# A transformer layer's start on one core: first loads, first modulation and first input stage in an order written by hand, and three router folds spread out

## The chip, the cores and the metric

The kernel runs on one core of one Trainium2 chip. Its engines are TensorE (PE in the rows, with its weight loads as PEld), VectorE (DVE), ScalarE (ACT), GpSimd (POOL) and SyncE (SP), which here only issues loads; 16 DMA engines move the data. The metric is the device time of one execution in microseconds, taken as the median of several runs.

## The reference

One layer works on x, 256 rows by 2048 columns, in float32, with a conditioning vector c of 2048:

```python
mod = silu(c) @ w_ada + b_ada                       # 6 vectors of 2048
shift1, scale1, gate1, shift2, scale2, gate2 = split(mod, 6)
h = layer_norm(x) * (1 + scale1) + shift1
q, k, v, su, sv, ga, gb = split(h @ w_in)           # 1024 columns each, ga and gb 2048
out_a = stick_breaking_attention(q, k, v)           # 8 heads of 128
out_b = gelu(su) * (mask(sgu_w) @ layer_norm(gelu(sv)) + sgu_b)
merged = sigmoid(ga) * (out_a @ w_proj_a) + sigmoid(gb) * (out_b @ w_proj_b)
x = layer_norm(alpha * x + gate1 * (merged @ w_out), ln1)
h = layer_norm(x) * (1 + scale2) + shift2
y = moe(h)    # 32 experts in 4 groups; one group, two of its experts for each row
return layer_norm(alpha * x + gate2 * y, ln2)
```

## The kernel before

All of it is one function, `trunk_kernel`, with helpers inside. Weights come in chunks of 128 x 2048 float32 (1 MB) through the tiles `ring` (four; in the input stages two more, `ringa`), each issued by `chunk` on SP's queue. SP and POOL issue in the order in which the code is written. PE, ACT and DVE get their order from a scheduler, up to the attention heads, where the order is written out too.

A product in float32 is made of three products of reduced parts (`mm3`, lines 203 to 205): `split` casts a chunk on ACT to the high part `wh` (line 194) and subtracts on DVE to the low part `wl` (line 195). `split_out` (lines 199 and 200) does the same with the transposed, modulated x, which becomes `hT`.

**Start.** `turn_x` loads the two halves of x, takes their statistics (line 161), normalizes them (line 182) and transposes them on PE by `pt` (line 187) into `nT`. Shift and scale of the first modulation come from chunks of w_ada in `ada_part`: the shift (`v` = 0) as a chain of multiply-adds into `comp` on DVE (lines 264 and 266), summed over partitions by PE's `pg<-ones` (line 274); the scale (`v` = 1) on PE, `pg<-ring,csg` (line 262), copied by ACT (line 271) and gathered by `pcols<-quart`. Both end with line 276 on DVE, which adds the bias column `bcol`. They are called `sh` and `sc` in the rows. Line 304 applies them to `nT`.

**Input projection.** `in_stage` runs over five groups of the 16 blocks of 128 in the inner dimension: (0, 1), (2, 3), 4 to 7, 8 to 11, 12 to 15. Each stage goes through five targets in turn, `sv` (kept in PSUM), `sut`, `qT`, `kT` and `vt`, with PSUM tiles `a` added to or copied to the target by `park` (lines 294 and 296). Between them it yields, and the caller pulls so many steps of the next stage's shift and scale as the tables PACE0 to PACE3 say:

```python
for kts, ahead, pace in (((0, 1), ada_half(1), PACE0), ((2, 3), ada_stage(1), PACE2), ...):
    for i, _ in enumerate(in_stage(kts)):
        pull(pace[i])
```

**After it** come spatial gating and attention, the two branch projections with their gates, the output projection into `y`, the norm, the routing and the experts, whose weights stream through the same tiles up to the end. In the output projection (16 chunks; group `g` of 4, step `q` of 4) three folds prepare the router's weights `wr`: `fold_shift` (lines 609 to 611: `pr<-sh,wr`, then wr times the scale), `fold_scale` (lines 616 to 618: `pr<-l1c,wr`, then wr times the norm's gain) and `fold_rows` (some transposes).

Of the kernel before, what the change touches and what calls it, by code (L numbers as in the profile page):

```python
# [9 lines left out]
F32R = mybir.dt.float32r  # L10
# [20 lines left out]
ADA3 = (2, 1, 0, 0, 1, 1, 0, 1, 1, 1)  # L31
ADAM = (1, 1, 1, 1, 1, 1, 1, 1, 2, 1, 1, 1, 1, 1, 1, 1)
ADAO = (1, 1, 1, 1)
PACE0 = (2, 2, 0, 0, 0, 0, 0, 0, 0, 0)
PACE1 = (1, 1, 1, 0, 1, 1, 1, 2, 1, 0)
PACE2 = (0, 2, 2, 1, 1, 0, 1, 1, 1, 0)
PACE3 = (1, 1, 2, 0, 2, 0, 1, 1, 1, 0)
# [6 lines left out]
def trunk_kernel(ctx, tc, x, c_t, w_ada1, w_ada2, b_ada, b_adac, w_in, sgu_wt, sgu_b, sgu_ln, w_pr, w_o, w_r, b_r,  # L44
# [9 lines left out]
    def m8(name, dt=F32):  # L54
        return wk.tile([128, D], dt, name=name, tag="m8", bufs=NM8)
# [40 lines left out]
    S.dma_start(cact, c_t)  # L96

    bcol = cp.tile([128, 6 * KT], F32, name="bcol")
    S.dma_start(bcol, b_adac)
    brc = cp.tile([36, 1], F32, name="brc")  # L100
    S.dma_start(brc, b_r)
    lnc = cp.tile([128, 2, G], F32, name="lnc")
    S.dma_start(lnc, sgu_ln)
    wr = cp.tile([128, KT, 36], F32, name="wr")
    S.dma_start(wr, w_r)
    l1c = cp.tile([128, 3, KT], F32, name="l1c")
    S.dma_start(l1c[:, 0:2], ln1_c)
    ones = cp.tile([128, 128], F32, name="ones")
    V.memset(ones, 1.0)
    V.memset(l1c[:, 2:3], 1.0)  # L110
# [40 lines left out]
    V.memset(ecol[0:1, 1:2], 1e6)  # L151
    csg = cp.tile([128, KT], F32, name="csg")
    S.activation(csg, cact, AF.Silu)
    V.tensor_scalar(bcol[:, KT:2 * KT], bcol[:, KT:2 * KT], 1.0, None, op0=ALU.add)
    V.tensor_scalar(bcol[:, 4 * KT:5 * KT], bcol[:, 4 * KT:5 * KT], 1.0, None, op0=ALU.add)


    def stats(parts, name):
# [12 lines left out]

    nT = [m8(f"nT{i}") for i in range(2)]

    def turn_x():
        X = []
        for n in range(NT):
            t = m8(f"x{n}")
            nc.sync.dma_start(t, x[n * 128:(n + 1) * 128])
            X.append(t)
        for n in range(NT):  # L180
            mv = stats(blocks(X[n]), f"x{n}")
            V.tensor_scalar(X[n], X[n], mv[:, 0:1], mv[:, 2:3], op0=ALU.subtract, op1=ALU.mult)
        for kp in range(8):
            pt = pb(f"pt{kp}")
            for k in range(2):
                for n in range(NT):
                    TE.transpose(pt[:, k * 256 + n * 128:k * 256 + (n + 1) * 128],
                                 X[n][:, (2 * kp + k) * 128:(2 * kp + k + 1) * 128], ident)
            S.copy(nT[kp // 4][:, (kp % 4) * 512:(kp % 4 + 1) * 512], pt)


    def split(w):
        wh, wl = w8("wh", F32R), w8("wl", F32R)
        S.copy(wh, w)  # L194
        V.tensor_sub(wl, w, wh)  # L195
        return wh, wl
# [15 lines left out]

    w_at = [0]

    def in_chunk():
        i = w_at[0]
        w_at[0] += 1
        return split(chunk(w_in[i]))

    def row_part(accs, parts, kts, w, c0, first, last):  # L220

# [26 lines left out]

    cols = {n: cp.tile([128, KT], F32, name=n) for n in ("sh1", "sc1", "sh2", "sc2")}

    def ada_part(v, src, k0, wd):

        pg = pb(f"pg{v}")
        comp = k2(f"comp{v}")[:, :wd]
        for i, a in enumerate(src):
            w = chunk(a)
            for k in range(D // wd):
                kt = D // wd * i + k
                col, ws = csg[:, kt:kt + 1], w[:, wd * k:wd * (k + 1)]
                if v == 1:  # L260
                    j = kt % 4
                    TE.matmul(pg[32 * j:32 * j + 32, :wd], col.to_broadcast([128, 32]), ws, start=kt < 4, stop=kt >= 12)
                elif kt == 0:
                    V.tensor_scalar(comp, ws, col, None, op0=ALU.mult)
                else:
                    V.scalar_tensor_tensor(comp, ws, col, comp, op0=ALU.mult, op1=ALU.add)
            if i < len(src) - 1:
                yield
        nb = wd // 128
        if v == 1:  # L270
            S.copy(comp, pg[:, :wd])
            pg = pb("pcols")
        for b in range(nb):
            TE.matmul(pg[:, b:b + 1], comp[:, b * 128:(b + 1) * 128], quart if v == 1 else ones[:, 0:1],
                      start=True, stop=True)
        V.tensor_add(cols["sc1" if v == 1 else "sh1"][:, k0:k0 + nb], pg[:, 0:nb],
                     bcol[:, v * KT + k0:v * KT + k0 + nb])
        yield

    def ada_half(f):  # L280
        for v in range(2):
            yield from ada_part(v, [w_ada1[v, 0, 2 * f + c] for c in range(2)], 2 * f, 256)

    def ada_stage(s):
        for v in range(2):
            yield from ada_part(v, [w_ada1[v, s, c] for c in range(4)], 4 * s, 512)

    vt, sut, qT, kT_ = m8("vt"), m8("sut"), m8("qT"), m8("kT")
    vtv = vt.rearrange("p (n c) -> p n c", n=NT)
    sva = [[pa(f"sv{g}{n}") for n in range(NT)] for g in range(2)]  # L290

# [6 lines left out]
    def in_stage(kts):  # L298

        w = D // len(kts)  # L300
        first, last = kts[0] == 0, kts[-1] == KT - 1
        for kt in kts:
            t = nT[kt // 8][:, (kt % 8) * 256:(kt % 8 + 1) * 256]
            V.tensor_scalar(t, t, cols["sc1"][:, kt:kt + 1], cols["sh1"][:, kt:kt + 1], op0=ALU.mult, op1=ALU.add)
            split_out(hT(hh, kt), hT(hl, kt), t)
        for dst in (None, sut, qT, kT_, vtv):
            for g in range(2):
                c0 = g * 512 % w
                if c0 == 0:
                    parts = in_chunk()  # L310
                if dst is None:
                    row_part(sva[g], parts, kts, w, c0, first, last)
                else:
                    accs = [pb(f"a{g}{n}") for n in range(2)]
                    if dst is vtv:
                        row_part(accs, parts, kts, w, c0, True, True)
                    else:
                        col_part(accs, parts, kts, w, c0)
                    for n in range(2):
                        park(dst[:, n, g * 512:(g + 1) * 512] if dst is vtv else  # L320
                             dst[:, (2 * g + n) * 512:(2 * g + n + 1) * 512], accs[n], first)
                yield
# [4 lines left out]
    def ada_steps():  # L327
        for v in (2, 3, 4, 5):
# [4 lines left out]
            for h in range(2):  # L333
# [19 lines left out]
                else:  # L353
                    for b in range(8):
                        TE.matmul(pg[:, b:b + 1], acc[:, 128 * b:128 * (b + 1)], ones[:, 0:1], start=True, stop=True)
                    V.tensor_add(cols["sh2" if v == 3 else "sc2"][:, 8 * h:8 * h + 8], pg[:, 0:8],
                                 bcol[:, v * KT + 8 * h:v * KT + 8 * h + 8])
                yield

    ada_it = ada_steps()  # L360
# [1 line left out]
    def ada_step(n=1):  # L362
        for _ in range(n):
            next(ada_it, None)

    turn_x()
    for _ in ada_half(0):
        pass

    def grow(extra):  # L370
        nonlocal ring
# [10 lines left out]
    def pull(n):  # L382
        for _ in range(n):
            next(ahead, None)

    more = [m8(f"ringa{i}") for i in range(NMORE)]
    grow(more)
    for kts, ahead, pace in (((0, 1), ada_half(1), PACE0), ((2, 3), ada_stage(1), PACE2),
                             (range(4, 8), ada_stage(2), PACE1), (range(8, 12), ada_stage(3), PACE3)):
        for i, _ in enumerate(in_stage(kts)):  # L390
            pull(pace[i])
    shrink(more)
    sgu = m8("sgu")
    wst = sgu[:, :1024].rearrange("p (g t) -> p g t", g=G)
# [231 lines left out]
    for g in range(4):  # L626
        accs = [pa(f"y{g}{n}") for n in range(NT)]
        for q in range(4):
# [6 lines left out]
                        wh[:, s], wl[:, s], kt == 0, kt == KT - 1)  # L635
            ada_step(ADAO[g])
            if g < 2 and q in (1, 3):
                (fold_shift, fold_scale, fold_rows, int)[2 * g + q // 2]()
        if g < 3:
            for n in range(NT):  # L640
                residual(g, n, accs[n])
# [573 lines left out]
```

## Time and profile before

| | |
|---|---|
| median of 3 runs | 1629.26 us (1628.90 to 1630.96) |
| profiled execution, its own time | 1632.55 us |
| its span | 1630.9 us |
| mean granted TensorE clock | 0.908 of full speed |
| busy: PE, PEld, DVE, ACT, POOL | 1382.5, 862.0, 808.5, 388.9, 56.6 us |
| DMA | 576.15 MB, mean 353 GB/s |

Times in rows count from the span's start. PE's busy time takes in matmuls that overlap, so it says where PE had work, not how fast it was. The shares are means over stages with different limits.

### The profile page before, as it was taken

Reading aid. Unit: us, or ns where it says so; the run is one execution under the profiler, and the core shown is the slowest. Engines: PE = TensorE matmul, PEld = TensorE weight load, DVE = VectorE, ACT = ScalarE, POOL = GpSimd, SP = SyncE. Lnnn points to the kernel's source line nnn. Section 1 sums busy time; section 2 is a strip of 40 time slices with the busy share of each in tenths; the row PEclk is TensorE's granted clock in tenths of the full one; section 3 lists DMA queues with packets and bytes.
Section 4 is the critical chain, followed back from the end, with each engine's and each line's share of the span. In section 5 each row is a group of like instructions: output and inputs, shape, how many; then the busy total and the mean of one; then the engine's idle time right before and its main releaser. Section 6 shows DMA issues by size and latency. Waiting matters only on the chain. (4 is left out here: it accounts for less than half of the span.)

```text
span 1630.9 us, 24878 instructions
## 1 busy us (share of the span) xinstructions
PE 1382.5 (85%) x10266; PEld 862.0 (53%) x10267; DVE 808.5 (50%) x1114; ACT 388.9 (24%) x521; POOL 56.6 (3%) x76
## 2 busy tenths in 40 slices
PE   4999999999999998994898698697697797797663
PEld 3879889898999996773423123133133133232111
DVE  6777879788788776877424113123123122132105
ACT  2522335564333332324201001001001001001002
POOL 0000000002000110000100000000000000000000
PEclk9899999999999998996999699799699799798777
DMA  8968878578989888883899999999999999999992
GB/s 323 356 255 315 335 275 302 178 246 310 347 321 338 318 309 333 309 340 163 342 421 420 422 421 420 422 421 420 421 420 421 421 421 421 421 420 421 421 421 123
DMA packets 80351, 576.15 MB, mean 353 GB/s; under 512 B 9448, under 2 KB 9448, under 8 KB 10600
## 3 DMA queue, kind: packets, MB, share of 16 engines
q1 hardware_dynamic: 78624, 569.41, 87.7%
q10 hardware_dynamic: 1608, 5.10, 0.8%
q8 instruction: 81, 1.33, 0.3%
q14 instruction: 38, 0.31, 0.0%
HBM read 572.38 MB, written 2.10 MB: 352 GB/s over the span
## 5 line engine op out<-in xcount | busy, mean ns | idle before, releaser
L195 DVE TENSOR_TENSOR wl<-ring,wh 128x2048 fp32r<-128x2048 f32 x95 | 217.6, 2292 | 25.8 <-ACT wh L194 25.7
L194 ACT CAST wh<-ring 128x2048 fp32r<-128x2048 f32 x95 | 180.9, 1906 | 148.3 <-DMA ring<-in_w_in 62.3
L937 DVE TENSOR_TENSOR hb<-sg,pgun 128x128 f32<-128x128 f32 x28 | 8.0, 287 | 329.8 <-ACT sg L936 329.8
L994 DVE TENSOR_TENSOR y<-pdn,comp 32x512 f32<-32x512 f32 x112 | 76.9, 687 | 186.7 <-PE pdn L973 185.5
L342 DVE SCALAR_TENSOR_TENSOR acc<-ring,csg,acc 128x1024 f32<-128x1024 f32 x120 | 153.6, 1280 | 6.1 <-DMA ring<-in_w_ada 4.5
L936 ACT ACTIVATE sg<-pgun 128x128 f32<-128x128 f32 x28 | 7.8, 277 | 610.6 <-PE pgun L930 610.6
L203 PE MATMUL a<-hT,wh 128*128 128x256 f32 x384 | 110.8, 289 | 0.0
L204 PE MATMUL a<-hT,wh 128*128 128x256 f32 x384 | 109.2, 285 | 0.0
L205 PE MATMUL a<-hT,wl 128*128 128x256 f32 x384 | 108.4, 286 | 0.0
L930 PE MATMUL pgun<-ringm,misc 128*32 128x256 f32 x1024 | 76.1, 437 | 17.6 <-DMA ringm<-in_w_gu 17.6
L1086 PE MATMUL po<-y,sl 128*128 128x512 f32 x112 | 64.2, 738 | 27.2 <-DVE sl L918 27.2
L930 PE MATMUL pgun<-ringw,misc 128*32 128x256 f32 x960 | 72.5, 441 | 16.8 <-DMA ringw<-in_w_gu 16.8
L930 PE MATMUL pgun<-ring,misc 128*32 128x256 f32 x992 | 69.9, 421 | 13.7 <-DMA ring<-in_w_gu 13.6
L205 PE MATMUL gb<-hT,wl 128*128 128x256 f32 x256 | 73.6, 287 | 7.5 <-DVE wl L195 7.5
L203 PEld LDWEIGHTS a<-hT,wh 128*128 128x128 f32 x384 | 74.5, 194 | 6.3 <-issue 3.6
L205 PEld LDWEIGHTS a<-hT,wl 128*128 128x128 f32 x384 | 73.8, 194 | 1.9 <-DVE sut L296 0.8
L204 PEld LDWEIGHTS a<-hT,wh 128*128 128x128 f32 x384 | 74.6, 194 | 0.4 <-issue 0.2
L205 PE MATMUL ga<-hT,wl 128*128 128x256 f32 x256 | 73.0, 285 | 1.1 <-DVE wl L195 1.1
L203 PE MATMUL ga<-hT,wh 128*128 128x256 f32 x256 | 72.8, 284 | 0.0
L203 PE MATMUL gb<-hT,wh 128*128 128x256 f32 x256 | 72.8, 284 | 0.0
L204 PE MATMUL gb<-hT,wh 128*128 128x256 f32 x256 | 72.4, 283 | 0.0
L204 PE MATMUL ga<-hT,wh 128*128 128x256 f32 x256 | 72.4, 283 | 0.0
(404 smaller groups left out, 2604.0 us busy)
## 6 DMA issues: line engine op xcount, KB each, us to landing
ring<-in_w_ada SPq DMA_DIRECT2D x87, 1024.0 KB, 5.9
ring<-in_w_gu SPq DMA_DIRECT2D x66, 1024.0 KB, 19.8
ringw<-in_w_gu SPq DMA_DIRECT2D x64, 1024.0 KB, 19.8
ringm<-in_w_gu SPq DMA_DIRECT2D x64, 1024.0 KB, 19.8
ring<-in_w_in SPq DMA_DIRECT2D x63, 1024.0 KB, 6.5
ringm<-in_w_down SPq DMA_DIRECT2D x32, 1024.0 KB, 19.9
ringw<-in_w_down SPq DMA_DIRECT2D x32, 1024.0 KB, 19.9
ring<-in_w_down SPq DMA_DIRECT2D x32, 1024.0 KB, 19.8
```

Source lines behind the costliest of these rows:

```text
L194: S.copy(wh, w)
L195: V.tensor_sub(wl, w, wh)
L203: TE.matmul(acc, lh, rh, start=first, stop=False)
L204: TE.matmul(acc, lh, rl, start=False, stop=False)
L205: TE.matmul(acc, ll, rh, start=False, stop=last)
L342: V.scalar_tensor_tensor(acc, ws, c, acc, op0=ALU.mult, op1=ALU.add)
L930: TE.matmul(acc[m * j:m * j + m, :2 * f].rearrange("p (a f) -> p a f", a=2), x[:, 2 * c + k], w[:, :, f * j:f * (j + 1)], start=i + k == 0 ...
L936: S.activation(sg[:, :w], acc[:, :w], AF.Silu)
L937: V.tensor_mul(hb[:, :w], sg[:, :w], acc[:, w:2 * w])
L994: V.tensor_mul(y4[32 * el:32 * el + 32, 512 * n:512 * (n + 1)], pdn[32 * n:32 * n + 32, :], gate2[0][32 * n:32 * n + 32, :])
L1086: TE.matmul(po, sl[:, n * 128:(n + 1) * 128], y4[:, 512 * b:512 * (b + 1)], start=True, stop=True)
```

## The change

The loads of `bcol`, `brc`, `lnc`, `wr` and `l1c` leave ACT's queue for SP's: `bcol` behind the first four chunks of w_ada, the others behind the first two chunks of w_in. These two chunks go to the tiles of `kT` and `vt`, which hold nothing yet (`early`). The 1 that was added to two sixths of `bcol` ahead of all is added at the end of each sum instead. From the work on x to the end of the first input stage, PE, ACT and DVE follow the order of the code (`begin`): chunk one of the shift, both chunks and the end of the scale, chunk two and the end of the shift. `in_stage` casts its first chunk before it modulates x and splits each next chunk one step ahead (`coming`); `ada_half` does the scale before the shift; PACE0 spreads the pulls. The folds move from the steps (g, q) = (0, 1), (0, 3), (1, 1) to (0, 1), (1, 1), (1, 3).

```diff
-PACE0 = (2, 2, 0, 0, 0, 0, 0, 0, 0, 0)
+PACE0 = (0, 1, 0, 1, 1, 1, 0, 0, 0, 0)
...
-    S.dma_start(bcol, b_adac)
-    S.dma_start(brc, b_r)
-    S.dma_start(lnc, sgu_ln)
-    S.dma_start(wr, w_r)
-    S.dma_start(l1c[:, 0:2], ln1_c)
...
-    V.tensor_scalar(bcol[:, KT:2 * KT], bcol[:, KT:2 * KT], 1.0, None, op0=ALU.add)
-    V.tensor_scalar(bcol[:, 4 * KT:5 * KT], bcol[:, 4 * KT:5 * KT], 1.0, None, op0=ALU.add)
...
-        return split(chunk(w_in[i]))
+        return split(early.pop(0) if early else chunk(w_in[i]))
...
-            w = chunk(a)
+            w = a if any(a is t for t in held.values()) else chunk(a)
...
-        V.tensor_add(cols["sc1" if v == 1 else "sh1"][:, k0:k0 + nb], pg[:, 0:nb],
-                     bcol[:, v * KT + k0:v * KT + k0 + nb])
+        V.scalar_tensor_tensor(cols["sc1" if v == 1 else "sh1"][:, k0:k0 + nb], pg[:, 0:nb], float(v == 1),
+                               bcol[:, v * KT + k0:v * KT + k0 + nb], op0=ALU.add, op1=ALU.add)
...
     def ada_half(f):
-        for v in range(2):
+        for v in (1, 0):
...
+        w0 = early.pop(0) if first else chunk(w_in[w_at[0]])
+        w_at[0] += 1
+        wh, wl = w8("wh", F32R), w8("wl", F32R)
+        S.copy(wh, w0)
         for kt in kts:
             t = nT[kt // 8][:, (kt % 8) * 256:(kt % 8 + 1) * 256]
             V.tensor_scalar(t, t, cols["sc1"][:, kt:kt + 1], cols["sh1"][:, kt:kt + 1], op0=ALU.mult, op1=ALU.add)
             split_out(hT(hh, kt), hT(hl, kt), t)
+        V.tensor_sub(wl, w0, wh)
+        coming, left = (wh, wl), 10 * 512 // w
         for dst in (None, sut, qT, kT_, vtv):
             for g in range(2):
                 c0 = g * 512 % w
                 if c0 == 0:
-                    parts = in_chunk()
+                    parts, left = coming, left - 1
+                    coming = in_chunk() if left else None
...
-    turn_x()
-    for _ in ada_half(0):
-        pass
...
+    nc.sync.dma_start(X[0], x[:128])
+    nc.sync.dma_start(X[1], x[128:])
+    held = {(v, c): chunk(w_ada1[v, 0, c]) for v, c in ((0, 0), (1, 0), (0, 1), (1, 1))}
+    nc.sync.dma_start(bcol, b_adac)
+    for t, src in ((kT_, w_in[0]), (vt, w_in[1])):
+        nc.sync.dma_start(t, src)
+        early.append(t)
+    begin = ExitStack()
+    begin.enter_context(tc.manual_schedule(engines={E.PE, E.Activation, E.DVE}))
+    turn_x()
+    shift, scale = [ada_part(v, [held[v, c] for c in range(2)], 0, 256) for v in range(2)]
+    next(shift)
+    next(scale)
+    next(scale)
+    next(shift)
+    nc.sync.dma_start(lnc, sgu_ln)
+    nc.sync.dma_start(wr, w_r)
+    nc.sync.dma_start(l1c[:, 0:2], ln1_c)
+    nc.sync.dma_start(brc, b_r)
     more = [m8(f"ringa{i}") for i in range(NMORE)]
     grow(more)
     for kts, ahead, pace in (((0, 1), ada_half(1), PACE0), ((2, 3), ada_stage(1), PACE2),
                              (range(4, 8), ada_stage(2), PACE1), (range(8, 12), ada_stage(3), PACE3)):
         for i, _ in enumerate(in_stage(kts)):
             pull(pace[i])
+        begin.close()
...
-                (fold_shift, fold_scale, fold_rows, int)[2 * g + q // 2]()
+                (fold_shift, int, fold_scale, fold_rows)[2 * g + q // 2]()
```

The changed kernel's lines are numbered a little lower (276 is 271 there, 262 is 257, 195 is 186). In the orders below a row is a line of the kernel, the operation, its output and inputs, and the output's shape; x8 counts equal rows, and the number behind a name tells one use of a tile from another. On DVE, from the shift's chain to the first stage's last low part, the order before is this (`comp_217` is the first shift, `comp_290` the next stage's):

```order
L266 SCALAR_TENSOR_TENSOR comp_217<-ring_66,csg,comp_217 128x256 x5
L266 SCALAR_TENSOR_TENSOR comp_217<-ring_67,csg,comp_217 128x256 x8
L276 TENSOR_TENSOR sh_132<-pg_216,bcol 128x2
L276 TENSOR_TENSOR sc_133<-pcols,bcol 128x2
L304 TENSOR_SCALAR nT_129<-nT_129,sc_133,sh_132 128x256 x2
L195 TENSOR_TENSOR wl<-ring_66,wh 128x2048
L200 TENSOR_TENSOR hT<-nT_129,hT 128x256 x2
L264 TENSOR_SCALAR comp_290<-ring_67,csg 128x256
L266 SCALAR_TENSOR_TENSOR comp_290<-ring_67,csg,comp_290 128x256 x7
L266 SCALAR_TENSOR_TENSOR comp_290<-ring_68,csg,comp_290 128x256 x8
L276 TENSOR_TENSOR sh_132<-pg_289,bcol 128x2
L195 TENSOR_TENSOR wl<-ringa_265,wh 128x2048
```

Now it is this (`comp_219` the first shift, `comp_426` the next; `kT` and `vt` here hold the first two chunks of w_in):

```order
L259 TENSOR_SCALAR comp_219<-ring_66,csg 128x256
L261 SCALAR_TENSOR_TENSOR comp_219<-ring_66,csg,comp_219 128x256 x7
L271 SCALAR_TENSOR_TENSOR sc_132<-pcols,bcol 128x2
L261 SCALAR_TENSOR_TENSOR comp_219<-ring_68,csg,comp_219 128x256 x8
L271 SCALAR_TENSOR_TENSOR sh_131<-pg_218,bcol 128x2
```

and from w1's low part on:

```order
L186 TENSOR_TENSOR wl<-vt,wh 128x2048
L186 TENSOR_TENSOR wl<-ring_67,wh 128x2048
L271 SCALAR_TENSOR_TENSOR sc_132<-pcols,bcol 128x2
L186 TENSOR_TENSOR wl<-ring_69,wh 128x2048
L259 TENSOR_SCALAR comp_426<-ringa_266,csg 128x256
L261 SCALAR_TENSOR_TENSOR comp_426<-ringa_266,csg,comp_426 128x256 x7
L261 SCALAR_TENSOR_TENSOR comp_426<-ringa_267,csg,comp_426 128x256 x8
L271 SCALAR_TENSOR_TENSOR sh_131<-pg_425,bcol 128x2
L302 TENSOR_SCALAR nT_122<-nT_122,sc_132,sh_131 128x256
```

`sc` has moved from behind all sixteen multiply-adds of the shift to between its eighth and its ninth, and the next shift's chain stands behind the next `sc` and the low parts of the third and fourth chunk.

On PE, at the end of the first stage's sv, the order before has the next stage's shift and scale ahead of the first `a`:

```order
L204 MATMUL sv_143<-wl,hT 128x512
L205 MATMUL sv_143<-wh,hT 128x512
L274 MATMUL pg_289<-ones,comp_290 128x1 x2
L262 MATMUL pg_324<-ring_69,csg 32x256 x8
L262 MATMUL pg_324<-ringa_264,csg 32x256 x8
L274 MATMUL pcols<-quart,comp_325 128x1 x2
L203 MATMUL a_354<-hT,wh 128x256
L204 MATMUL a_354<-hT,wh 128x256
```

Now the first group of scale stands there alone, and the matmuls of `sut` follow at once:

```order
L195 MATMUL sv_138<-wl,hT 128x512
L196 MATMUL sv_138<-wh,hT 128x512
L257 MATMUL pg_306<-ring_66,csg 32x256 x8
L194 MATMUL a_322<-hT,wh 128x256
L195 MATMUL a_322<-hT,wh 128x256
L196 MATMUL a_322<-hT,wl 128x256
```

The rest of that scale now stands between the matmuls of `sut` and `qT`, and `pg<-ones` between those of `qT` and `kT`.

At the folds PE had this before:

```order
L570 MATMUL pe<-comp_1992,ident 128x512 x3
L609 MATMUL pr_5768<-sh_134,wr 36x1 x16
L616 MATMUL pr_5851<-l1c,wr 36x3 x16
L203 MATMUL y_5702<-wh,mh_3211 128x512
L203 MATMUL y_5703<-wh,mh_3211 128x512
```

Now the first of these is followed by `y` at once, and the other stands here, some 120 rows on:

```order
L194 MATMUL y_5860<-wh,mh_3212 128x512
L194 MATMUL y_5861<-wh,mh_3212 128x512
L349 MATMUL pg_5923<-acc_5554,ones 32x512 x2
L636 MATMUL pr_5927<-l1c,wr 36x3 x16
L195 MATMUL y_5860<-wl,mh_3212 128x512
```

`pr<-l1c` has moved from ahead of the third chunk's matmuls to the middle of a later group's.

## Rows read from the trace of the kernel before

**Rows 1.** The page of the profile: the engines' busy time, and of the 40 slices of 40.8 us the granted TensorE clock, the DMA engines' share and what they moved.

```profile
PE 1382.5 (85%) x10266; PEld 862.0 (53%) x10267; DVE 808.5 (50%) x1114; ACT 388.9 (24%) x521; POOL 56.6 (3%) x76
...
PEclk9899999999999998996999699799699799798777
...
DMA  8968878578989888883899999999999999999992
...
GB/s 323 356 255 315 335 275 302 178 246 310 347 321 338 318 309 333 309 340 163 342 421 420 422 421 420 422 421 420 421 420 421 421 421 421 421 420 421 421 421 123
```

**Rows 2.** Busy time by stretch of 20 us: stretch, its length, then for PE, PEld, DVE, ACT and POOL busy time and instructions, granted clock, DMA share, GB/s.

```profile
60.00:80.00 20.00, 20.00 (x127) 18.11 (x126) 17.15 (x19) 11.09 (x13) 0.00 (x0) 1.00 0.84 309
...
280.00:300.00 20.00, 18.07 (x120) 16.26 (x119) 19.17 (x34) 7.12 (x11) 0.00 (x0) 1.00 0.71 255
...
660.00:680.00 20.00, 19.46 (x90) 15.03 (x89) 18.73 (x17) 7.51 (x4) 0.00 (x0) 1.00 0.89 316
...
760.00:780.00 20.00, 14.90 (x73) 10.24 (x73) 12.73 (x32) 5.86 (x5) 0.95 (x1) 0.68 0.17 58
...
800.00:820.00 20.00, 18.93 (x222) 7.51 (x218) 5.99 (x11) 4.99 (x10) 0.62 (x1) 0.91 1.01 424
```

**Rows 3.** Timeline of the start: start, duration, engine, line, operation, out<-in, count, and in brackets the idle time before it and what ended it.

```profile
9.05 0.17 DVE L154 TENSOR_SCALAR bcol<-bcol 128x16 f32<-128x16 f32 x1 [7.41 <-DMA bcol<-in_b_adac]
...
9.21 2.47 DVE L161 BATCH_NORM_STATS2 st_x<-x 128x6 f32<-128x512 f32 x4
...
18.28 6.73 DVE L266 SCALAR_TENSOR_TENSOR comp<-ring,csg,comp 128x256 f32<-128x256 f32 x13
...
18.42 5.00 PE L187 MATMUL pt<-ident,x 128*128 128x128 f32 x28 [1.49 <-DVE x L182]
...
25.16 0.75 PE L274 MATMUL pg<-ones,comp 128*128 128x1 f32 x4 [1.74 <-DVE comp L266]
...
25.84 3.38 PE L262 MATMUL pg<-ring,csg 128*32 128x256 f32 x32
...
29.30 0.37 ACT L271 COPY comp<-pg 128x256 f32<-128x256 f32 x1 [5.12 <-PE pg L262]
...
29.72 0.61 PE L274 MATMUL pcols<-quart,comp 128*128 128x1 f32 x4 [0.50 <-ACT comp L271]
...
30.63 0.74 DVE L304 TENSOR_SCALAR nT<-nT,sc,sh 128x256 f32<-128x256 f32 x2
```

**Rows 4.** All instructions on the tiles x, of the first 30 us: the two loads with their issue (durations in ns; first and last start), and the time from issue to landing.

```profile
L178 SPq DMA_DIRECT2D x<-in_x x2: 386/406/426, 0.8 to 1.3; - x2
...
DMA to landing us min/median/max: 5.2/6.4/7.6
```

**Rows 5.** Timeline of the first input stage, columns as in rows 3.

```profile
33.85 1.22 PE L204 MATMUL sv<-wl,hT 128*128 128x512 f32 x2 [0.28 <-DVE wl L195]
...
39.14 0.39 PE L205 MATMUL sv<-wh,hT 128*128 128x512 f32 x1
...
42.22 1.90 ACT L194 CAST wh<-ringa 128x2048 fp32r<-128x2048 f32 x1 [10.14 <-DMA ringa<-in_w_in]
...
42.69 0.98 PE L274 MATMUL pg<-ones,comp 128*128 128x1 f32 x4 [3.16 <-DVE comp L266]
...
43.60 1.93 PE L262 MATMUL pg<-ring,csg 128*32 128x256 f32 x16
...
47.73 1.01 PE L274 MATMUL pcols<-quart,comp 128*128 128x1 f32 x4 [0.49 <-ACT comp L271]
```

**Rows 6.** PE alone by stretch: stretch, length, busy time and instructions, granted clock, DMA share, GB/s.

```profile
25.80:29.30 3.50, 3.42 (x33) 0.57 0.97 323
...
43.00:52.00 9.00, 8.51 (x56) 0.50 0.98 382
...
53.00:60.00 7.00, 7.00 (x61) 1.00 0.99 399
```

**Rows 7.** Timeline of the second input stage on DVE (first two) and PE, and of PE at the third stage's first matmul.

```profile
64.02 2.29 DVE L195 TENSOR_TENSOR wl<-ring,wh 128x2048 fp32r<-128x2048 f32 x1 [1.68 <-ACT wh L194]
...
66.23 4.68 DVE L266 SCALAR_TENSOR_TENSOR comp<-ringa,csg,comp 128x512 f32<-128x512 f32 x6
...
81.55 0.95 PE L274 MATMUL pg<-ones,comp 128*128 128x1 f32 x8
...
82.36 0.36 PE L203 MATMUL a<-hT,wh 128*128 128x256 f32 x1
...
85.40 1.06 PE L262 MATMUL pg<-ring,csg 128*32 128x512 f32 x8
...
87.07 1.04 PE L262 MATMUL pg<-ringa,csg 128*32 128x512 f32 x2
...
111.01 0.61 PE L203 MATMUL sv<-wh,hT 128*128 128x512 f32 x2
```

**Rows 8.** Timeline around the second fold, in the output projection.

```profile
630.82 0.74 DVE L611 TENSOR_TENSOR wr<-wr,sc 128x576 f32<-128x576 f32 x1
...
631.71 2.05 PE L616 MATMUL pr<-l1c,wr 128*36 128x3 f32 x32 [4.82 <-DVE wr L611]
...
634.54 4.48 DVE L195 TENSOR_TENSOR wl<-ring,wh 128x2048 fp32r<-128x2048 f32 x2
...
636.87 0.80 PE L204 MATMUL y<-wl,mh 128*128 128x512 f32 x1 [1.96 <-DVE wl L195]
```

More of the change, by code (lines that the diff above doesn't have):

```diff
@@ L172, in trunk_kernel @@
     nT = [m8(f"nT{i}") for i in range(2)]
+    X = [m8(f"x{n}") for n in range(NT)]
+    vt, sut, qT, kT_ = m8("vt"), m8("sut"), m8("qT"), m8("kT")
     def turn_x():
[L175 to L179, printed above, removed]
         for n in range(NT):
@@ L213, in trunk_kernel @@
     w_at = [0]
+    early = []
     def in_chunk():
@@ L249, in trunk_kernel @@
     cols = {n: cp.tile([128, KT], F32, name=n) for n in ("sh1", "sc1", "sh2", "sc2")}
+    held = {}
     def ada_part(v, src, k0, wd):
@@ L286, in ada_stage @@
             yield from ada_part(v, [w_ada1[v, s, c] for c in range(4)], 4 * s, 512)
-    vt, sut, qT, kT_ = m8("vt"), m8("sut"), m8("qT"), m8("kT")
     vtv = vt.rearrange("p (n c) -> p n c", n=NT)
@@ L355, in ada_steps @@
                         TE.matmul(pg[:, b:b + 1], acc[:, 128 * b:128 * (b + 1)], ones[:, 0:1], start=True, stop=True)
-                    V.tensor_add(cols["sh2" if v == 3 else "sc2"][:, 8 * h:8 * h + 8], pg[:, 0:8],
-                                 bcol[:, v * KT + 8 * h:v * KT + 8 * h + 8])
+                    V.scalar_tensor_tensor(cols["sh2" if v == 3 else "sc2"][:, 8 * h:8 * h + 8], pg[:, 0:8],
+                                           float(v == 4), bcol[:, v * KT + 8 * h:v * KT + 8 * h + 8],
+                                           op0=ALU.add, op1=ALU.add)
                 yield
```

## The prediction

> **What bounds the kernel now.** I read the page's totals and slices first, then busy time by stretch, and last the timelines of the start, of the second stage and of the fold. TensorE is busy 85% of the span and VectorE 50% [rows 1], but neither is the bound everywhere. At 60 to 80 us PE is busy all 20.00 us and DVE 17.15; at 280 to 300 DVE has 19.17 of 20 and PE 18.07; at 660 to 680 both are near full; at 800 to 820 the DMA engines are (share 1.01, 424 GB/s), and the page's line of slices shows them so from there to the end [rows 1, 2]. Between lies the routing (760 to 780), where the DMA share is 0.17 [rows 2]: the expert loads wait there for the routing's answer, so they cannot swallow a delay ahead of it. What moves the routing by 1 us therefore moves the end by about 1 us, and what moves PE's stream of the in-stages, when it has no slack to give, moves the routing. DVE must be looked at by stage: wherever it holds 17 us or more of 20, an instruction put ahead of another is a delay.
>
> A measurement of this kernel tells a change from none at about 0.2%, 3.3 us. Sums below are against the profiled execution, 1632.55 us by its own time; the median of the runs is 1629.26, and I carry the difference over to that.
>
> **The loads that move.** The five small loads leave ACT's queue. The two DVE instructions that read `bcol` held DVE: it waited 7.41 us, to 9.05, with x behind it [rows 3]. x0 was issued at 0.8 and landed 5.2 us later, at 6.0 [rows 4]. So DVE begins its statistics at about 6.1 instead of 9.21, 3.1 us earlier. On SP's queue `bcol` stands behind two x and four 1 MB chunks; at the 323 GB/s of the first slice [rows 1] these 6.3 MB take 19.5 us, and it is first needed at about 25: covered with some 5 us. w_in[0] and w_in[1] follow by 23 to 27 and are needed from 32 on; their new tiles add no copy. The other four loads are wanted hundreds of us later. All this costs nothing; were the cover of `bcol` gone, the first stage would slip by as much.
>
> **The start, instruction by instruction.** Statistics and norm of x1, behind which the multiply-adds went on at 18.28 [rows 3], end at about 15.0 (3.1 earlier; the norm's own chain through ACT takes what the three multiply-adds between no longer do). 32 transposes take 1.09 + 5.00 = 6.1 (the first four lie just ahead of the row shown; 28 took 5.00 [rows 3]), to 21.1. Scale's 32 pg matmuls took 3.38 [rows 3] at a granted clock of 0.57 over 25.8 to 29.3 [rows 6]; at full they would take about 1.9; I take 2.6, to 23.7. ACT's copy 0.37, pcols 0.61, the waits between: `sc` is ready at 25.1. Now DVE: its first 8 multiply-adds (0.518 each, 6.73 for 13 [rows 3]) are done at 18.9, and the next one in its order is `sc`. **It stands still for 6 us**, then does the other eight, 4.1, to 29.2. pg<-ones 0.75, `sh` 0.2, and nT begins at 30.2 against 30.63: what the earlier x gave is eaten by the place of `sc`. nT, cast and low part come twice in turn ahead of w0's low part (0.37 each, three engines' steps in a row, 2.3 us), then wl 2.29 [rows 7], to 34.9. Before, PE went on at 33.85 with 4 of the 24 sv done [rows 5]; now at 35.0 with one done. The 20 took 5.68 (33.85 to 39.53 [rows 5]), 0.284 each; 23 take 6.5, to 41.5.
>
> Here comes the gain. Before, PE then waited 3.16 for DVE, and ACT waited 10.14 for w1, to 42.22 [rows 5]. Now w1 was early, so `sut`'s 48 matmuls go at once. 24 took 3.04 (82.36 to 85.40 [rows 7]); 48 take 6.1. With two groups of pg (0.97 each, half of 1.93 for 16), copy 0.5 and pcols 1.0 the mark "pcols done" stands at 51.1, against 48.74 before [rows 5], but with 48 matmuls more behind it: PE is ahead by some 4 us of work.
>
> **The end of the first stage.** DVE's order is `sc`, w3's low part, then all 16 multiply-adds of the next shift. ACT casts w3 behind its copy, 50.1 to 52.0; wl to 54.3; sixteen at 0.518 (0.35 for the first), 8.1, to 62.4. PE has done qT's 48 by 57.2 and its next instruction is pg<-ones: a wait of about 5 us that before was not there, since the shift came from chunks pulled in earlier. It eats the lead: pg<-ones ends at 63.4.
>
> **The second stage** hangs on DVE, not on PE. From 63.4: sh 0.2, nT 0.74, low parts 0.75, two wl 4.6, to 69.6; then 16 multiply-adds of 512 (0.48 + 15 x 0.78, from 4.68 for six), 12.2; two more wl 4.6; two sut sums 1.4; one wait for ACT's cast as the 1.68 [rows 7]: 89.5. PE, there at 81.55 before [rows 7], comes some 2.4 later (the mark 2.4 later, 6.1 of its work done, 5.1 waited, 1.0 for pg<-ones, the lower clock after the wait about as long as before), at 84, and waits some 5 us. The matmul behind pg<-ones, at 82.36 before [rows 7], comes at 90.3: **+7.9**. Two interruptions of 1.04 us each, where pg<-ringa split in three [rows 7], are one piece now: -2.1. The granted clock after a wait: behind the 3.16 us it was 0.50 (the 1.2 GHz level) for 43 to 52, and 1.00 at 53 to 60 [rows 6]. What that costs after the two new waits I bound by 0 and by such a stretch, 4.5; I take 1.3, since here 6 to 20 us of unbroken work lie ahead of each wait, where at 39.5 PE had only just begun. So the third stage (sv at 111.01 [rows 7]) starts +7.1 later.
>
> **The folds.** At 631.71 PE waited 4.82 for DVE's wr, did pr<-l1c in 2.05, and then waited 1.96 for wl, which DVE could do only after two small operations, at 634.54 [rows 8]. Without fold_scale there, wl follows wr at 631.5: -3.0. fold_scale comes later, where PE is full: about +1.0 for its matmuls at full clock. I take -2.0; the bounds are 0 (DVE is at 18.73 of 20 there [rows 2], so its work may simply be late next) and -3.0. fold_rows moves behind it, with the same operations; nothing waits for it there.
>
> The new form of the sums with bias (scalar_tensor_tensor for tensor_add) has no row; it is between nothing and the 0.1 more of a small operation, ten times: nothing taken.
>
> **Sum.** +7.9 +1.3 -2.1 -2.0 = +5.1, so 1637.7 for a profiled execution and **1634.4** as a median. Bounds: without ACT's wait (-1.7), full clock for pg (-0.9), no loss after waits (-1.3) and -3.0 for the folds it is +0.2; with half clock for a whole stretch (+3.2) and in pg (+0.8), folds at 0 (+2.0), +11.1.
>
> **Rivals.** *More.* The clock stays at the lower level behind both waits as at 43 to 52 [rows 6]: 1638.5 to 1641. For it: that row. Against: one such stretch in so many us of work.
>
> *The same.* The third stage or a later one has slack that takes the lag in; With half the +7.1 gone the sum is +1.5; 1627 to 1632. For it: at 280 to 300 PE has 18.07 of 20, so it waits there already, and a PE that comes late would wait less if DVE's own row came no later. Against: DVE's row holds the sums of PE's results, so it is late with PE, and PE has no slack at 60 to 80 [rows 2]. The Trainium skill ("Perfetto Trace Analysis", section Identifying the Most-Contended Engine) judges which engine limits a kernel by its occupancy over the trace; by that PE at 85% is the limit, a new order on DVE at 50% is free, and the time would be 1629.3. The stretches above disagree here: DVE has 17.15 of 20.
>
> *Faster.* The two waits of PE don't come. DVE is idle from about 35 to 50, and the 16 multiply-adds fit there if their chunks and their turn allow. Then wl w3 ends at 54.3, sh follows at once, DVE is at the next pg<-ones by 80.4, PE's next matmul at 81.2: -1.2 -2.1 -2.0 = -5.3, 1624; if PE waits in neither place, its lead stands whole, -3.5 -2.1 -2.0 = -7.6, 1621.7. It decides below about 4 us for the two waits together. Against: `sc` and w3 stand ahead of them in DVE's row, and the 7.41 us that DVE waited for `bcol`, with x0 landed at 6.0 [rows 3, 4], show that it passes nothing. The Trainium skill ("TensorE: Matmul & The Clock Gate", section on the 16x 32x32 array, queue depths) says so as a rule: ACT and DVE take their queues strictly in order. The trace agrees, by those 7.41 us.
>
> **Chances.** Forecast, 1632.6 to 1638.5: 0.55. More: 0.13. The same: 0.20. Faster: 0.12. Slower by over 0.2% (above 1632.5): 0.68. The range leaves out "faster" and the far end of "more": 1628 to 1641, held by what hangs between.
>
> **What will show it.** Right: DVE idle about 6 us at 19 to 25 before `sc`; nT near 30; sut's matmuls begun near 42; PE idle about 5 us before pg<-ones near 57 to 62 and again near 84 to 90; sv of the third stage near 118; the wait for wl at the folds gone, about 2 us of the lag given back. Wrong: the multiply-adds of the next shift done before 57, `sc` ready as early as DVE's eighth multiply-add, or loads of w0 and w1 landing after 33; then the sums above have no ground.

## The result: slower, by more than twice the forecast, and the profile after

The changed kernel takes 1642.68 us (median of 5 runs, 1638.65 to 1645.58) against 1630.96 us of the kernel before in the same comparison (5 runs, 1628.90 to 1632.81): a ratio of 1.0072, 95% interval 1.0053 to 1.0091, 11.7 us more. The forecast was slower, 1634.4, with a range that ended at 1641.0. It was +5.1 on a median of three runs, 1629.26; over the five runs of the comparison the kernel before has 1630.96, so 1.7 of the 8.3 us between 1634.4 and 1642.68 are this base, and 6.6 are the change. A further comparison of the same two kernels gave 1.0067 (1.0050 to 1.0083).

The profiled execution of the changed kernel took 1645.58 us, 13.0 more than that of before (1632.55). Its page, with busy time, granted clock and DMA share in the form of [rows 1]:

```profile
PE 1389.3 (85%) x10266; PEld 869.1 (53%) x10267; DVE 808.3 (49%) x1112; ACT 387.7 (24%) x519; POOL 56.7 (3%) x76
...
PEclk8999999999999988997999799799699698698766
...
DMA  9787968568889888875799999999999999999992
```

The totals do not tell the cause: PE is busy 7 us longer, at a lower clock. The rows that the forecast named do. The start, columns as in [rows 3] (line 261 is the multiply-add, 257 scale's pg, 271 the end of `sc` and `sh`, 302 the modulation):

```profile
15.58 3.61 DVE L261 SCALAR_TENSOR_TENSOR comp<-ring,csg,comp 128x256 f32<-128x256 f32 x7
...
20.78 1.93 PE L257 MATMUL pg<-ring,csg 128*32 128x256 f32 x32
...
23.85 0.16 DVE L271 SCALAR_TENSOR_TENSOR sc<-pcols,bcol 128x2 f32<-128x2 f32 x1 [4.67 <-PE pcols L269]
...
23.95 4.13 DVE L261 SCALAR_TENSOR_TENSOR comp<-ring,csg,comp 128x256 f32<-128x256 f32 x8
...
29.51 0.41 DVE L302 TENSOR_SCALAR nT<-nT,sc,sh 128x256 f32<-128x256 f32 x1
...
43.31 0.38 PE L194 MATMUL a<-hT,wh 128*128 128x256 f32 x1
```

DVE's first eight multiply-adds end at 19.2, then it stands 4.67 us for `sc` (forecast 6); nT begins at 29.51, 1.1 us earlier than in [rows 3], and `sut`'s first matmul goes at 43.31 (forecast 30.2 and 42). The end of the first stage, the second, and the first sv of the third:

```profile
51.45 0.16 DVE L271 SCALAR_TENSOR_TENSOR sc<-pcols,bcol 128x2 f32<-128x2 f32 x1 [12.81 <-PE pcols L269]
...
52.59 2.29 DVE L186 TENSOR_TENSOR wl<-ring,wh 128x2048 fp32r<-128x2048 f32 x1 [0.98 <-ACT wh L185]
...
55.18 7.25 DVE L261 SCALAR_TENSOR_TENSOR comp<-ringa,csg,comp 128x256 f32<-128x256 f32 x14
...
63.11 0.99 PE L269 MATMUL pg<-ones,comp 128*128 128x1 f32 x4 [5.83 <-DVE comp L261]
...
89.79 1.83 PE L269 MATMUL pg<-ones,comp 128*128 128x1 f32 x8 [4.69 <-DVE comp L261]
...
91.48 0.56 PE L194 MATMUL a<-hT,wh 128*128 128x256 f32 x1
...
119.09 0.39 PE L194 MATMUL sv<-wh,hT 128*128 128x512 f32 x1
119.31 0.39 PE L195 MATMUL sv<-wl,hT 128*128 128x512 f32 x1
```

Before, behind the first sv at 111.01 [rows 7]:

```profile
112.67 0.50 PE L204 MATMUL sv<-wl,hT 128*128 128x512 f32 x1 [1.04 <-DVE wl L195]
```

PE waits 5.83 us before the first pg<-ones and 4.69 before the second (forecast some 5 for each). The matmul behind it comes at 91.48 (forecast 90.3, before 82.36 [rows 7]) and the third stage starts at 119.09, 8.1 later than the 111.01 of [rows 7] (forecast 7.1). Part of these 8.1 is gone at once: before, PE waited 1.04 us there for wl, which it does not now, so the first `sv<-wl` is only 6.6 later (119.31 against 112.67). The fold:

```profile
642.44 0.74 DVE L631 TENSOR_TENSOR wr<-wr,sc 128x576 f32<-128x576 f32 x1
...
643.11 4.48 DVE L186 TENSOR_TENSOR wl<-ring,wh 128x2048 fp32r<-128x2048 f32 x2
...
645.44 0.80 PE L195 MATMUL y<-wl,mh 128*128 128x512 f32 x1 [2.37 <-DVE wl L186]
```

wl now follows wr at once, as forecast; against [rows 8] the first wait of 4.82 is gone and the second, 1.96, is 2.37.

### The profile page after: what moved, and what is told of

The parts are those of the page before. It is cut to its first block, busy times and chain, and to the rows that moved or that the text cites. A ratio compares the mean times of both kernels' runs of the same rounds, so it can differ in the third digit from the quotient of the medians.

```text
span 1643.9 us, 24872 instructions
## 1 busy us (share of the span) xinstructions
PE 1389.3 (85%) x10266; PEld 869.1 (53%) x10267; DVE 808.3 (49%) x1112; ACT 387.7 (24%) x519; POOL 56.7 (3%) x76
## 5 line engine op out<-in xcount | busy, mean ns | idle before, releaser
L186 DVE TENSOR_TENSOR wl<-ring,wh 128x2048 fp32r<-128x2048 f32 x89 | 203.9, 2292 | 26.8 <-ACT wh L185 26.8
L185 ACT CAST wh<-ring 128x2048 fp32r<-128x2048 f32 x89 | 169.5, 1906 | 135.7 <-DMA ring<-in_w_o 45.8
L950 PE MATMUL pgun<-ringm,misc 128*32 128x256 f32 x1024 | 79.8, 453 | 20.0 <-DMA ringm<-in_w_gu 20.0
```

The lines of the kernel that those rows point to most:

```text
L950: TE.matmul(acc[m * j:m * j + m, :2 * f].rearrange("p (a f) -> p a f", a=2), x[:, 2 * c + k], w[:, :, f * j:f * (j + 1)], start=i + k == 0 ...
```

## The experiments

Times are ratios, with their 95% interval, and differences of medians against the kernel before, run in turn on the same chip. The numbers given for the third stage are the start of its first sv in the run's profile, set against the changed kernel's first profile (119.09). w0 to w3 are the first chunks of w_in; the lag of an instruction is how much later it starts than the same instruction of the kernel before.

**Folds alone.** The kernel before with one line changed:

```diff
-                (fold_shift, fold_scale, fold_rows, int)[2 * g + q // 2]()
+                (fold_shift, int, fold_scale, fold_rows)[2 * g + q // 2]()
```

> The kernel before with the folds alone moved. Theory (the changed kernel's loss is the first two input stages' order; the folds gain a little): PE's wait for wl at the first y goes, y starts 4 to 5 us earlier, but some 3.4 us of it are given back through the output projection, as the lag of the changed kernel grew there from 8.2 to 11.6: -1.3 (-3.0 to 0) against the kernel before. Rival (moving the folds is itself a loss, since DVE is full there): y starts earlier and the routing comes at least 1 us later, +1 to +3.

Measured 0.9984 (0.9969 to 0.9998), -2.1 us by the medians (1630.29 and 1632.35). DVE and PE at the fold:

```profile
628.52 0.74 DVE L611 TENSOR_TENSOR wr<-wr,sc 128x576 f32<-128x576 f32 x1
...
629.19 4.48 DVE L195 TENSOR_TENSOR wl<-ring,wh 128x2048 fp32r<-128x2048 f32 x2
...
631.52 0.79 PE L204 MATMUL y<-wl,mh 128*128 128x512 f32 x1 [3.44 <-DVE wl L195]
```

The first y with wl comes 2.3 us behind wl's start, with no pr<-l1c ahead. In the traces the lag falls by 5.0 us at the first y, and 3.5 of that are given back by the end of the output projection (the two further folds now stand in two later steps, (1, 1) and (1, 3)): -1.5. The theory holds, the rival falls. This is the only version whose interval lies below the kernel before, if barely.

**Old folds in the changed kernel.**

```diff
-                (fold_shift, int, fold_scale, fold_rows)[2 * g + q // 2]()
+                (fold_shift, fold_scale, fold_rows, int)[2 * g + q // 2]()
```

> The changed kernel with the folds where they were. Theory: +0 to +3 against the changed kernel, so +11.7 to +14.7 against the kernel before. Rival (the folds cost): below the changed kernel, +9 to +11 against the kernel before.

1.0075 (1.0054 to 1.0095), +11.4 by the medians, against +10.1 and +11.7 of the changed kernel: nothing that can be told apart, which fits 1.5 either way. The loss is not in the folds; the third stage starts at 120.52 here. Up to the folds this is the changed kernel, so its trace is a further profile of that part: the granted clock falls near 300 as it does there, but not near 582 and 610, where the changed kernel's other profiles have it (last series below).

**The first shift whole ahead of `sc`.** `ada_part` gets a further pause behind its last chunk, and the calls change, so that the second call does the second chunk and the last one pg<-ones and `sh`:

```diff
-    next(shift)
-    next(scale)
-    next(scale)
-    next(shift)
+    next(shift)
+    next(shift)
+    next(scale)
+    next(scale)
+    next(shift)
```

> The changed kernel with all sixteen multiply-adds of the first shift ahead of the end of the first scale on DVE. Theory: DVE no longer stands still before sc, nT begins near 25.1 instead of 29.5, and since everything behind hangs on that chain, PE's two waits for the next shifts stay and the third stage starts 4.4 earlier than in the changed kernel: +2.3 at the third stage and some +7 in all against the kernel before. Rival (the chain through the loads decides, and w0 or w1 is late): nT earlier, but sv starts where it did, gain below 1.5 us.

1.0037 (1.0022 to 1.0052), +5.4. DVE's `sc` and nT, and PE at the end of the first stage:

```profile
24.30 0.16 DVE L271 SCALAR_TENSOR_TENSOR sc<-pcols,bcol 128x2 f32<-128x2 f32 x1 [0.83 <-PE pcols L269]
...
25.01 0.41 DVE L302 TENSOR_SCALAR nT<-nT,sc,sh 128x256 f32<-128x256 f32 x1
...
57.86 0.99 PE L269 MATMUL pg<-ones,comp 128*128 128x1 f32 x4 [5.83 <-DVE comp L261]
```

DVE waits 0.83 instead of 4.67, nT begins at 25.01, 4.5 earlier, and the wait of 5.83 before pg<-ones is there unchanged, 5.2 earlier. Third stage 115.67, 3.4 earlier than the changed kernel. The standing still before `sc` is worth 3.4 us at the third stage, of the 4.4 that were expected, and the loads of w0 and w1 do not bind.

**The next shift ahead of its scale.** `ada_half` goes over v = 0, 1 (with the pause), and

```diff
-PACE0 = (0, 1, 0, 1, 1, 1, 0, 0, 0, 0)
+PACE0 = (0, 1, 1, 1, 1, 1, 0, 0, 0, 0)
```

> The changed kernel with the next stage's shift pulled ahead of its scale, its multiply-adds behind the low parts of w1 and w2, in DVE's idle time. Theory: PE's 5.8 us wait at 57 to 63 goes with the lower clock behind it, the second stage's DVE chain starts some 8 us earlier, PE's wait before its second pg<-ones shrinks below 3 us, and the third stage starts 6 to 9 earlier than in the changed kernel, +0 to -2 against the kernel before; in all +2 to +5 against the kernel before. Rival (the second stage is late by its own DVE work): the first wait goes, the second grows by as much, and less than 2 us are gained.

1.0039 (1.0024 to 1.0055), +7.1. The next `sh` and `sc` on DVE, and PE's second pg<-ones:

```profile
49.49 0.16 DVE L273 SCALAR_TENSOR_TENSOR sh<-pg,bcol 128x2 f32<-128x2 f32 x1 [2.23 <-PE pg L271]
...
58.62 0.16 DVE L273 SCALAR_TENSOR_TENSOR sc<-pcols,bcol 128x2 f32<-128x2 f32 x1 [4.76 <-PE pcols L271]
...
85.27 0.99 PE L271 MATMUL pg<-ones,comp 128*128 128x1 f32 x4 [7.05 <-DVE comp L261]
```

`sh` comes at 49.49 instead of 64.13 and the first wait of PE is gone: the second stage starts 6.9 us earlier than in the changed kernel. But the second wait grew from 4.69 to 7.05, so that the third stage starts only 3.4 earlier (115.68), between the theory (6 to 9) and the rival (under 2). The rival had the half of it that I had left out: the second stage is late by DVE's own work, whose chain begins behind `sc` at 58.62, only 5.5 earlier than behind `sh` at 64.13 in the changed kernel.

**Both together**, as a further edit of the same two places.

> Both reorderings of the first stage together (all of the first shift ahead of the first scale's end; the next stage's shift ahead of its scale). Theory: nT near 25, no wait of PE at the end of the first stage, second stage (first sv) 7 to 8 earlier than before; the second stage is still late by DVE's own multiply-adds of the shift after next, so about half of that is lost at its pg<-ones: third stage -1 against the kernel before, all in all -4 to +1 with the folds and the later stretches of lower clock. Rival (PE's waits only move): third stage +3 as in each reordering alone, +6 in all.

0.9996 (0.9984 to 1.0008), -1.0 by the medians; third stage 108.90, 10.2 earlier than the changed kernel. That is more than the two alone, 3.4 each; why it is more is not shown. The loss of the change is undone by order alone, with its loads, its splits ahead and its folds all in place.

**And the shift after next later.**

```diff
-PACE2 = (0, 2, 2, 1, 1, 0, 1, 1, 1, 0)
+PACE2 = (0, 1, 1, 1, 1, 1, 1, 1, 1, 0)
```

> As the one before, and PACE2 of the second stage from (0, 2, 2, 1, 1, 0, 1, 1, 1, 0) to (0, 1, 1, 1, 1, 1, 1, 1, 1, 0): pg<-ones of the shift after next stands 48 matmuls later on PE. Theory: the second wait of PE goes too (DVE done near 82, PE there near 80), the third stage -5 to -8 against the kernel before, all in all -5 to -10, faster than both kernels. Rival (the DVE chain is late wherever it is waited for): the wait moves and stays 4 to 5 us, no better than the one before.

0.9998 (0.9987 to 1.0010), -0.7; third stage 107.60. PE's wait is 48 matmuls later and still 5.69 us, against 7.04 in the run before: the rival holds, the wait mostly moves.

**The loads alone.** The kernel before with the five loads on SP's queue (`bcol` here ahead of the first four chunks) and the bias sums in their new form.

```diff
-    S.dma_start(bcol, b_adac)
...
+    nc.sync.dma_start(bcol, b_adac)
     for _ in ada_half(0):
         pass
+    nc.sync.dma_start(lnc, sgu_ln)
...
```

> The kernel before with the five small loads on SP's queue (bcol behind x, the others behind the first four chunks) and the sums with bias in their new form, nothing else moved: PE, ACT and DVE are ordered by the scheduler. Theory: DVE starts on x 3 us earlier, that reaches nT and sv, and since nothing stands in its way the third stage and the end are 2 to 3 earlier: -2 to -3. Rival (w0, behind the same ring tiles, sets the start): below 1 us.

1.0017 (1.0006 to 1.0027), +2.7, the wrong sign for the theory. nT, ACT's cast of w0 and the first sv:

```profile
25.86 0.74 DVE L297 TENSOR_SCALAR nT<-nT,sc,sh 128x256 f32<-128x256 f32 x2
...
26.94 1.89 ACT L187 CAST wh<-ring 128x2048 fp32r<-128x2048 f32 x1
...
28.88 1.65 PE L196 MATMUL sv<-wh,hT 128*128 128x512 f32 x3 [3.33 <-ACT wh L187]
...
45.17 1.89 ACT L187 CAST wh<-ringa 128x2048 fp32r<-128x2048 f32 x1
...
47.12 0.58 PE L196 MATMUL a<-hT,wh 128*128 128x256 f32 x1 [3.30 <-ACT wh L187]
```

nT is 4.8 earlier than in [rows 3], and 3.0 earlier than in the three later profiles of before (28.81 to 28.97), whose scale was not slowed. But w_in[0] goes through a ring tile and its cast begins at 26.94: PE waits 3.33 for it and begins sv only 1.1 to 1.3 earlier than those three (30.00 to 30.16). So without the tiles of `kT` and `vt` most of the earlier x is lost at w0, as the rival has it. The rest is lost at w1, which the rival had not named: its cast goes at 45.17, behind the next modulation on ACT, and PE waits 3.30 for it; before it began at 42.22 [rows 5]. The third stage starts at 109.95, inside the range of before (105.03 to 111.01). What makes the whole 2.7 us longer is not shown; this profile has the two falls of the clock, near 574 and 601, of which the last series tells.

**The changed kernel once more.**

> The changed kernel once more, unaltered, for a second profile. Theory: +6 to +8 at the third stage again, since that hangs on order and durations; the further steps of its first profile (1.7 at 298 us, 1.5 at 581, 2.6 at 609), each at a stretch of granted clock 0.50 where the kernel before had 1.00, come at other places or not at all. Rival (these steps belong to the change, by a wait that it moves): the same places, the same sizes.

1.0067; third stage 118.48. The stretches of lower clock near 298, 581 and 609 came again, so the rival stood, until the last series below.

**The kernel before once more, and pure delays.** The delays stand at the first gate of the heads, with the order of PE, DVE and ACT otherwise the same; here the longest of 24, 40 and 60 matmuls:

```diff
+        for _ in range(60 if name == "ga0" else 0):
+            TE.matmul(acc, wh[:, :128], hT(hh, 0), start=True, stop=True)
```

> The kernel before once more, unaltered, for a second profile. Theory (a wait of PE that every kernel has lowers the granted clock in some positions and not in others): no stretch of 0.50 between 60 and 620 us, as in its first profile, if the positions hold from run to run; rival (chance in each run): such stretches after the 1.7 us wait near 571 or near 600, in this profile as in the one of the loads alone.

> The kernel before with 24 further matmuls of 256 columns on PE at the start of the first head's gate (near 305 us), order else the same on PE, DVE and ACT: 24 x 0.118 = 2.8 us of pure delay. Theory: the delay itself arrives at 570 whole, and what comes on top is a fall of the clock behind waits that are unchanged (1.5 us near 571, 2.6 near 600, or none): between +2.8 and +7. Rival (later waits take the delay in): +0 to +2.

> As the one before, with 40 matmuls, 4.7 us of pure delay. Theory: +4.7 to +9, by the falls near 571 and 600. Rival (later waits take the delay in): +0 to +3.

> As the one before, with 60 matmuls, 7.1 us of pure delay, about what the changed kernel has lost at its third stage. Theory: +7.1 to +11.5, by the falls near 571 and 600. Rival (later waits take the delay in): +3 to +5.

The kernel before gave 0.9992 (0.9979 to 1.0005), third stage 107.87, and no stretch of 0.50 between 60 and 620. The delays gave 1.0005 (0.9992 to 1.0019), 1.0021 (1.0009 to 1.0034) and 1.0024 (1.0011 to 1.0037): +1.6, +3.7 and +5.1 by the medians. The longest, in its trace:

```profile
302.94 7.43 PE L243 MATMUL ga<-hT,wh 128*128 128x256 f32 x60
```

7.3 us to the next matmul, of which 6.2 arrive behind the heads (one wait took in 1.0). By the medians 2.8 us of delay cost 1.6, 4.7 cost 3.7 and 7.1 cost 5.1 (at most 6.0 by the interval). The shortest lies in the rival's range, the other two between rival and theory: later waits do take some of a delay in. That falls of the clock come with a delay as such is not borne out: one of the three traces had one, near 598.

**Two more profiles of each kernel, in turn on one chip.**

> The kernel before, a third profile, on the same chip as the next three. If the stretches of granted clock 0.50 behind the unchanged waits near 571 and 600 come by chance in any kernel: one of the two profiles of before in this series has one of them. If they belong to the changed kernel: none in either.

> The changed kernel, a third profile. By chance: at least one of the stretches near 581 and 609 is missing in one of the two profiles of this series. If they belong to the kernel: 0.50 near 298, 581 and 609 in both, 13 +- 1 behind the first profile of before at the end.

> The kernel before, a fourth profile, as e13. The start of its first profile (scale's 32 matmuls in 3.38 us at 0.57) should not come again if it was chance: 1.93 at full clock here and in e13.

> The changed kernel, a fourth profile, as e14. The fall near 298 should be there in each profile of this kernel, since the wait ahead of it is longer here (2.41 us, against 1.34 in before).

The start of the third stage in all eight profiles (us):

| | first | second | third | fourth | mean |
|---|---|---|---|---|---|
| before | 111.01 | 107.87 | 105.03 | 108.75 | 108.2 |
| changed | 119.09 | 118.48 | 119.54 | 120.50 | 119.4 |

PE alone by stretch, columns as in [rows 6]. First the changed kernel's first profile:

```profile
296.00:304.00 8.00, 5.51 (x23) 0.79 0.51 171
...
581.00:586.00 5.00, 4.44 (x24) 0.66 0.72 244
...
609.00:617.00 8.00, 8.00 (x36) 0.57 0.61 227
```

The same places of the program in the first profile of before:

```profile
289.00:297.00 8.00, 7.11 (x39) 1.00 0.67 242
...
572.00:577.00 5.00, 4.19 (x35) 1.00 0.68 229
...
598.00:606.00 8.00, 8.00 (x61) 1.00 0.76 264
```

In the third of before (its first row is scale's pg at the start):

```profile
24.00:28.00 4.00, 2.44 (x36) 1.00 0.73 240
...
566.00:571.00 5.00, 4.46 (x24) 0.66 0.71 249
...
594.00:602.00 8.00, 8.00 (x36) 0.57 0.63 239
```

And in the third of the changed kernel:

```profile
296.00:304.00 8.00, 6.40 (x28) 0.79 0.51 178
...
581.00:586.00 5.00, 4.29 (x35) 1.00 0.71 246
...
609.00:617.00 8.00, 8.00 (x54) 0.79 0.65 211
```

Single times were 1632.24 and 1629.64 us for before, 1643.29 and 1644.61 for the changed kernel. The fall near 298 is in all four profiles of the changed kernel (and in the one with old folds) and in none of before: it comes with the change. The two later ones are not its own: the third profile of before has both, 0.66 and 0.57, to the hundredth what the changed kernel has, behind the same waits, and the third of the changed kernel lacks the first and has the second at half its length. Their count is 7 of 8 places in the changed kernel and 2 of 8 in before; with the profiles of the two runs on the folds, which are alike up to there and have none, 7 of 10 and 2 of 10. That leaves open whether they come more often in the changed kernel. And scale's pg, at 0.57 in [rows 6], ran at 1.00 in each later profile of before.

## Why the prediction was right in its mechanism and wrong in its size

**The loads, right.** x came 3.2 us earlier, `bcol`, w0 and w1 in time; the loads-only run shows that without the new tiles most of this is lost at w0.

**DVE's order, right.** Each mark of the first two stages came within 1.3 us of its number, and the two reorderings took the loss away: 5.4 and 7.1 us of loss were left with one, none with both. That DVE passes nothing held: it stood 4.67 us and 12.81 us for the two `sc`, and in the reorderings the multiply-adds that had stood behind ran in that time. The marks were in part luck: scale's pg took 1.93 us for the 2.6 taken and `sc` was 1.3 early, while the 23 sv put at 6.5 took 8.0 (34.30 to 42.31), since the granted clock was 0.50 from 26.1 to 39.8; the two errors nearly cancel.

**The third stage, right against the same profile**: +8.1 at the first sv and +6.6 at the first `sv<-wl`, for +7.1. The clock fell behind both new waits as in the rival "more":

```profile
60.00:67.00 7.00, 3.89 (x18) 0.52 0.77 283
...
87.00:95.00 8.00, 5.21 (x27) 0.57 0.87 330
```

The first stretch costs little, since DVE binds there; behind the second, pg<-ones alone took 1.83 for the 0.95 of before, and the matmuls behind it ran at 0.50 up to 94.4. An estimate from this is 2.3 us (0.9 for pg<-ones and half of the 2.9 from 91.5 to 94.4), so 1.3 for both was too little by 1.0. The reason given for 1.3, unbroken work ahead of each wait, is not borne out by these two stretches. The matmul behind pg<-ones was 9.1 late, forecast 7.9; the wait for wl that only the kernel before has took 1.4 back at the third stage.

**The step that failed: "Sums below are against the profiled execution ... and I carry the difference over."** That profile of before was a late one. Its third stage starts at 111.01, against 108.2 for the mean of four and 107.2 for the other three. Of these 3.8 us, 1.7 came at the start, where its scale matmuls ran at 0.57 and took 3.38 where they take 1.93 (nT at 30.63, in the other three at 28.81 to 28.97). The rest came in the first stage, where 0.50 was granted for 10.2 us from 42.5 on, of which [rows 6] shows 43 to 52; in the third profile, the earliest, there is no such stretch (1.00 over 39 to 50). I read one execution's clock as the kernel's. Against the mean the change costs 119.4 - 108.2 = 11.2 at the first sv, and 119.6 - 109.8 = 9.8 at the first `sv<-wl`, where before has its wait behind it; not 8.1 and 6.6. The profiled 1632.55 stood 3.3 us above the median of 1629.26, but the whole time alone would not have told: the third profile took 1632.24 with the earliest third stage of all. The stretch of 0.57 in [rows 6] could have.

**What the sum left out: the clock at 298.** Past the hand-ordered part the scheduler orders ACT otherwise, though the diff does not touch that place. After, on ACT, DVE and PE:

```profile
295.77 1.90 ACT L185 CAST wh<-ring 128x2048 fp32r<-128x2048 f32 x1 [6.03 <-DMA ring<-in_w_in]
...
298.01 0.76 DVE L191 TENSOR_TENSOR obl<-mix,obh 128x256 fp32r<-128x256 f32 x2 [1.63 <-ACT obh L190]
...
299.56 1.22 PE L454 MATMUL pm<-sgu,sv 128*128 128x128 f32 x4 [2.41 <-DVE mix L456]
```

Before, ACT alone:

```profile
290.40 0.41 ACT L199 CAST obh<-mix 128x256 fp32r<-128x256 f32 x1 [4.90 <-DVE mix L439]
...
290.71 1.90 ACT L194 CAST wh<-ring 128x2048 fp32r<-128x2048 f32 x1
```

Before, `obh`'s cast stands ahead of the next weight cast; after, that cast, which waited 6.03 for its load, holds `obh` and through it DVE (1.63) and PE (2.41). The clock falls there, and the lag grows by 1.0 to 1.8 in the four profiles, while before's own does not. I had let the lag stand unchanged from the third stage on. Why the clock falls there stays open. In the four reorderings of the first stage ACT has the same order at this place and PE waits 1.17 to 1.77 us (1.53 to 2.52 in the changed kernel's four profiles), and the clock stays at 1.00 and the lag does not grow. Those four have a fall near 224 to 232 instead, where PE waits 1.36 for ACT's `comp`; the changed kernel has that wait too, and no fall behind it. So neither the order nor the length of the wait is enough.

**The folds, right:** -1.5 for -2.0.

So 9.8 + about 1.4 - 1.5 = 9.7, against +10.1 and +11.7 by the medians. The rest is not settled. The later falls near 581 and 609 cost 1.5 and up to 3.0 us when they come; by their count and length in the eight profiles they would add, as an estimate, some 2.3 to the changed kernel, to 12.0, and the profiled executions themselves differ by 13.3 (means of four, 1644.7 and 1631.4). How often they come in the other runs is not known. Both are in the profile of 1645.58, 2.9 above its median. The rival "more" came true as a mechanism, at 1.0 us instead of the 4 that it was priced at; the late profile and the fall at 298 were in no case of the prediction. "The same" did not come: DVE was busy 49% of the span, and its order in two stages cost the time all the same.

## What to carry to other kernels

Before a sum is set against a profile, see whether that execution is a typical one: look for stretches of lower granted clock in just the stage that the change rebuilds, and take a second profile where there are any. What one execution lost there is no property of the kernel, and its whole time alone does not show it. A hand order of one engine must be read as a queue: an instruction that waits for another engine (here `sc`, for PE) belongs behind the work that is ready, and moving it pays in full only when the next wait on that chain is moved too (3.4 us for either alone, 10.2 for both). And where a scheduler orders what follows, a change upstream reorders it: compare the orders there as well.

## What the runs showed of the hardware that was not expected

The same wait can be followed by a fall of the granted clock in one execution and not in another of the same kernel: gb's wait of 1.7 us for wl near 570 in the kernel before was followed by full clock in three profiles and by 0.50 in one, at a cost of 1.5 us; the stretch at 598 to 606 has no wait of PE inside, only small matmuls, and ran at 1.00 in three and at 0.57 in one, at 3.0. In the reorderings the 1.36 us wait for ACT near 224 to 232 was followed by a fall in all four, and in the changed kernel in none. Executions of the kernel before differ by up to 11 us in one comparison (1626.4 to 1637.7); how much of that is such falls is not shown.
